# Up projection set up ahead of ten token tiles of the output projection, sample attention behind them

## The chip, the cores and the metric

The kernel runs on one core of a Trainium2 chip. The time is device microseconds (us) of that core for one execution. The kernel before took 2938.07 us, the median of 3 runs (2932.61 to 2941.27).

## What is computed

One decoder layer on 2064 prompt tokens (2048 and 16 learned ones ahead of them) and 32 sample tokens (8 sequences of 4, each with 2048 cached tokens in pages). Cut to what matters here:

```
q, k, v, u = split(rmsnorm(x, norm1) @ w_in)
ssm  = glu(S5(u))                                  # 512 columns
attn = head_norm(diff_attention(q, k, v))          # 512 columns, prompt
attn_sample = head_norm(diff_attention(q, [cache_k[pages], k], [cache_v[pages], v]))
x  = x + concat(attn, ssm) @ w_out                 # 1024 x 1024
xn = rmsnorm(x, norm2)
h  = gelu(causal_dwconv3(xn @ w_gate)) * (xn @ w_up)   # 1024 -> 2816, twice
y  = x + h @ w_down
```

All in float32: each large product is made of three matmuls over two fp32r parts of each operand (`mm3`, L80 to L82), so one operation of the text above is three PE instructions.

## The kernel before

The 2096 tokens lie in 17 tiles of 128 rows. Tile 16 has the last 48: 16 prompt tokens and the 32 sample tokens. The program is written stage by stage in `run` (L1580 ff.), and a scheduler (`schedule_with_timeline_sim=True`) puts the instructions of each engine in order: what is written earlier has priority, and what is written later is moved ahead where its own simulation finds an engine free and the buffers of the later stage are there. So the order in the text of `run`, and which pool of buffers opens where, set the order of the work. The pools lie in two stacks, one on each side of the memory, and a pool that takes the place of an earlier one waits for what was in it.

The stages that the change touches, in the order of the kernel before:

- `attend`, the prompt's attention, with work of lower priority beside it: `out_ssm` (the SSM half of the output projection of all tiles), `out_setup` (weights of the attention half, by `load_w_out`, L1111) and `out_attention(range(6))`, the other half for tiles 0 to 5.
- `out_attention(range(6, 16), ahead=True)`, the ten tiles 6 to 15, in pools of their own: `oax` with two buffers of each tile and `oap` with four banks of PSUM. A token tile takes two steps. `out_heads` (L1185 to L1208) loads three parts (`oxt`, and `ot` twice), multiplies and splits them on POOL and ACT, does 24 matmuls into two PSUM tiles `po` and stores the sum. `out_norm` (L1210 to L1240) norms it (`normed`, L161, with the scratch tile `xs`), transposes it (`tp`), and stores quarters of it and their differences in `XB`, from which the up projection reads. With `ahead` the norm of a tile is written behind the heads of the next.
- `up_setup` and `load_up` (L1288 ff.), which begin `ffn_up`: products `g` of tokens `xb` and weights `uw` (raw weights `uraw`), 128 columns of features a unit, 22 units in each of three blocks of token tiles: 0 to 5, 6 to 11, 12 to 16. A unit has seven products of quarter matrices (Strassen-Winograd), 12 matmuls each. A block cannot begin before all its tiles are in `XB`; the third needs tile 16.
- `sample_attention`, whose pools `smc` and `smw` open ahead of the ten tiles. It fetches the cache by gathers that POOL issues (L607): tiles `kv`, three buffers, 128 x 1024 float32 each, 64 gathers of keys and 64 of values. Keys are transposed on PE (`tps`), split and multiplied with the queries; after each half of the keys comes a softmax (`Ss`, L656 ff.); values are split by ACT (`vh`, L686) and DVE (`vl`, L688) and multiplied; the heads' sums (`att`, L699) are normed, transposed and put into `OT`, where tile 16 reads them.
- `out_setup` again, for tile 16, and `out_attention([16])`: the weights are loaded once more, in halves of 512 columns, each `oraw` through the one buffer with the tag "ot".
- `ffn_up`, which in the order of the engines runs beside the sample attention and tile 16, then `ffn_down`.

## Time and profile before

| | |
|---|---|
| median of 3 runs | 2938.07 us (2932.61 to 2941.27) |
| profiled execution, its own time | 2936.48 us |
| its span | 2934.7 us |
| granted clock of PE, mean of the span | 0.973 |
| PE (matmul) busy | 2750.9 us, 94% |
| PEld (weight load) busy | 2364.0 us, 81% |
| DVE busy | 2225.7 us, 76% |
| ACT busy | 1403.3 us, 48% |
| POOL busy | 1000.8 us, 34% |

Times inside the execution are us from the start of the span. A granted clock of 1.00 is the full 2.4 GHz of PE. Busy shares are means over the span: stages differ, so the table by stretches, further down, says more. L163 is line 163 of the kernel before; `po<-owh,oa` is an instruction that writes tile po and reads owh and oa. "x4" is a count, ACTq or SP a queue from which transfers are issued, "tile: min/median/max" are durations in ns.

### The profile page before, as it was taken

The page shows a single profiled execution, that of the slowest core. Times are in us where ns is not written, and L with a number is a line of the kernel's source. Part 1 is how long each engine was busy: PE and PEld are TensorE (multiplying, and loading weights), DVE is VectorE, ACT ScalarE, POOL GpSimd, SP SyncE. Part 2 cuts the span into 40 slices and gives each one's busy share as a digit, 9 for nine tenths or more (in the row PEclk, how much of TensorE's full clock was granted, in tenths as well). Part 3 has the DMA queues.
Part 4 walks back from the last instruction along what each step waited for, and adds up shares of the span by engine and source line. Part 5 has one row for each costly group of instructions (what it writes and reads, how often), then busy time and mean ns, then how long its engine had stood idle before and what let it go on. Part 6 is the DMA issues. An engine that isn't in the chain of part 4 may idle for free.

```text
span 2934.7 us, 43647 instructions
## 1 busy us (share of the span) xinstructions
PE 2750.9 (94%) x14916; PEld 2364.0 (81%) x14916; DVE 2225.7 (76%) x4317; ACT 1403.3 (48%) x2859; POOL 1000.8 (34%) x1381
## 2 busy tenths in 40 slices
PE   6989989979999899787999999999999998999999
PEld 6966667867887777676998998988999997778776
DVE  6748876757678898557898878898889994675566
ACT  3323223545556666335566556665565562222234
POOL 4525442115445576564243432343214441000000
PEclk9999999989999999999999999999999999999999
DMA  7876776977864332587455546454454447676554
GB/s 224 255 194 149 205 216 168 236 216 195 230 182 141 116 113 83 166 266 228 156 161 186 160 145 213 145 181 159 133 168 130 127 125 290 216 245 195 178 190 132
DMA packets 452553, 529.73 MB, mean 181 GB/s; under 512 B 91546, under 2 KB 353578, under 8 KB 451305
## 3 DMA queue, kind: packets, MB, share of 16 engines
q1 hardware_dynamic: 360584, 385.75, 45.0%
q10 hardware_dynamic: 72848, 72.79, 7.5%
q0 software_dynamic: 18896, 68.39, 7.4%
q8 instruction: 118, 1.93, 0.3%
q14 instruction: 107, 0.87, 0.1%
HBM read 390.49 MB, written 135.14 MB: 179 GB/s over the span
## 4 chain that ended last, share of the span: by engine, by line
PE 55%; DVE 9%; DMA 8%; POOL 2%; issue 2%; ACT 2%; SPq 0%; ACTq 0%; POOLq 0%; DVEq 0%
PE g L80 8%; PE g L81 8%; PE g L82 8%; PE pq L80 4%; PE pq L81 4%; PE pq L82 4%; PE O L537 3%; DVE p L507 2%; DMA ot<-RR 2%; PE po L80 1%; DMA oraw<-in_w_out_dram 1%; DMA dt<-MT 1%; PE po L81 1%; PE po L82 1%; PE tps L632 1%
## 5 line engine op out<-in xcount | busy, mean ns | idle before, releaser
L80 PE MATMUL g<-xb,uw 128*128 128x384 f32 (+1 forms) x1848 | 594.0, 324 | 8.8 <-DVE A L1408 4.8
L81 PE MATMUL g<-xb,uw 128*128 128x384 f32 (+1 forms) x1848 | 595.8, 323 | 1.2 <-DVE xb L69 1.2
L82 PE MATMUL g<-xb,uw 128*128 128x384 f32 (+1 forms) x1848 | 584.7, 322 | 0.4 <-DVE uw L69 0.4
L80 PEld LDWEIGHTS g<-xb,uw 128*128 128x128 f32 x1848 | 346.8, 188 | 19.3 <-DVE A L1408 5.3
L81 PEld LDWEIGHTS g<-xb,uw 128*128 128x128 f32 x1848 | 347.9, 188 | 9.1 <-issue 2.3
L82 PEld LDWEIGHTS g<-xb,uw 128*128 128x128 f32 x1848 | 346.1, 188 | 7.0 <-issue 1.2
L475 ACT ACTIVATE p<-S,nms 128x484 f32<-128x484 f32 (+11 forms) x360 | 210.1, 589 | 157.6 <-DVE nms L474 136.0
L80 PE MATMUL pq<-dw,da 128*128 128x512 f32 x616 | 245.9, 401 | 19.6 <-ACT da L68 11.8
L69 DVE TENSOR_TENSOR uw<-uraw,uw 128x512 fp32r<-128x512 f32 x330 | 239.5, 734 | 26.7 <-ACT uw L68 24.7
L68 ACT ACTIVATE uw<-uraw 128x512 fp32r<-128x512 f32 x330 | 201.0, 625 | 114.6 <-PE g L82 77.2
L81 PE MATMUL pq<-dw,da 128*128 128x512 f32 x616 | 245.5, 399 | 0.0
L82 PE MATMUL pq<-dw,da 128*128 128x512 f32 x616 | 236.9, 398 | 0.0
L474 DVE TENSOR_REDUCE nms<-S 128x1 f32<-128x484 f32 (+11 forms) x360 | 190.9, 554 | 40.9 <-PE S L469 27.4
L68 ACT ACTIVATE da<-dt 128x1024 fp32r<-128x1024 f32 x66 | 69.8, 1058 | 249.4 <-PE pq L82 149.3
L95 POOL TENSOR_TENSOR rs_y<-rs_v,half 128x8 f32<-128x8 f32 (+4 forms) x77 | 105.8, 1377 | 243.9 <-DVE rs_v L90 225.9
L80 PE MATMUL pj<-wh,x 128*128 128x512 f32 (+1 forms) x408 | 170.6, 419 | 8.1 <-ACT wh L74 5.7
L81 PE MATMUL pj<-wl,x 128*128 128x512 f32 (+1 forms) x408 | 170.3, 417 | 2.7 <-DVE wl L75 2.6
L82 PE MATMUL pj<-wh,x 128*128 128x512 f32 (+1 forms) x408 | 169.6, 416 | 0.0
L468 PE MATMUL S<-kt,qs 128*128 128x484 f32 (+11 forms) x360 | 145.7, 407 | 23.3 <-ACT p L475 13.5
L1311 POOL TENSOR_TENSOR uraw<-uraw 128x512 f32<-128x512 f32 x66 | 108.0, 1637 | 160.6 <-DVE s L1309 112.4
L80 PEld LDWEIGHTS pq<-dw,da 128*128 128x128 f32 x616 | 117.2, 190 | 50.5 <-ACT da L68 12.7
L505 POOL TENSOR_TENSOR p<-p,g 128x412 f32<-128x412 f32 (+13 forms) x164 | 156.5, 983 | 3.4
(423 smaller groups left out, 6895.7 us busy)
## 6 DMA issues: line engine op xcount, KB each, us to landing
dt<-MT SPq DMA_DIRECT2D x99, 512.0 KB
uraw<-in_w_gate_dram SPq DMA_DIRECT2D x66, 512.0 KB
uraw<-in_w_up_dram SPq DMA_DIRECT2D x66, 512.0 KB
raw<-in_w_in_dram SPq DMA_DIRECT2D x80, 256.0 KB
MT<-z ACTq DMA_DIRECT2D x44, 384.0 KB
dT<-in_w_down_dram SPq DMA_DIRECT2D x66, 256.0 KB
qs<-QST SPq DMA_DIRECT2D x128, 128.0 KB
draw<-in_w_down_dram SPq DMA_DIRECT2D x55, 256.0 KB
```

The costliest lines, as they stand in the source:

```text
L68: nc.scalar.activation(hi, src, AF.Copy)
L69: nc.vector.tensor_tensor(out=lo, in0=src, in1=hi.bitcast(F32), op=ALU.subtract)
L80: mm(out, lhsT=lh, rhs=rh, start=start, stop=False, skip_group_check=goes_on)
L81: mm(out, lhsT=lh, rhs=rl, start=False, stop=False, skip_group_check=goes_on)
L82: mm(out, lhsT=ll, rhs=rh, start=False, stop=stop, skip_group_check=goes_on)
L95: nc.gpsimd.tensor_tensor(out=y, in0=v, in1=e, op=ALU.pow)
L468: nc.tensor.matmul(dst, lhsT=qs[:, 0, c, qa : qa + M], rhs=kt[c][:, x:y], start=True, stop=False)
L474: nc.vector.tensor_reduce(out=nms[:M, z : z + 1], in_=dst, axis=AX.X, op=ALU.max, negate=True)
L475: nc.scalar.activation(p[:M, Z + x : Z + y], dst, AF.Exp, bias=nms[:M, z : z + 1], accum_out=sms[:M, z : z + 1])
L505: nc.gpsimd.tensor_tensor(out=pw[1][:M, x], in0=pw[1][:M, x], in1=g[:M, z : z + 1].to_broadcast([M, x.stop - x.start]), op=ALU.mult)
L537: nc.tensor.matmul(O[:, :N], lhsT=v, rhs=tw[:, m - a, :N], start=(m == 0), stop=(m == nb))
L1311: gp.tensor_tensor(out=a21, in0=a11, in1=a21, op=ALU.subtract)
```

## The change

The stages are written in another order: after the attention stand `up_setup`, with its pools and the products' PSUM, then the ten token tiles, and then the sample attention, whose pools `smc` and `smw` now open behind the ten tiles. The ten tiles use a pool with one buffer of each tile (`oax`, 1) and the PSUM pool of the up projection (`psf`) in place of one of their own. To make room the scratch tiles of the norm share buffers: `xs` and `xt1` with `ot`, `xod` with `oa`; the weights of both halves of the output projection share the buffers `owh0` to `owh3` and `owl0` to `owl3`, in one pool `oac` on the right. The option `ahead` is gone: a tile's norm is written right behind its heads. Nothing is computed in another way.

```diff
--- before.py
+++ after.py
@@ -61,6 +61,7 @@
 class Step:
     def __init__(self, tc, ins, outs):
         self.tc, self.nc, self.i, self.o = tc, tc.nc, ins, outs
+        self.tags = {"xs": "xs", "xod": "xod"}
     def split(self, hi, lo, src):
@@ -161,7 +162,7 @@
     def normed(self, wp, xt, n, g):
         nc = self.nc
-        xs = wp.tile([P, D], F32, name="xs", tag="xs")
+        xs = wp.tile([P, D], F32, name="xs", tag=self.tags["xs"])
         ss = wp.tile([P, 1], F32, name="ss", tag="ss")
         nc.scalar.activation(xs[:n], xt[:n], AF.Square, accum_out=ss[:n])
         r = self.rsqrt(wp, ss[:n], [n, 1], 1.0 / D, EPS, "xr")
@@ -1116,8 +1117,8 @@
         for k in range(k0, k0 + H):
             raw = wp.tile([P, n], F32, name="oraw", tag="ot")
             nc.sync.dma_start(out=raw, in_=i["w_out"][0, k * P : (k + 1) * P, c])
-            a = cp.tile([P, n], F32R, name="owh", tag=f"owh{k}")
-            b = cp.tile([P, n], F32R, name="owl", tag=f"owl{k}")
+            a = cp.tile([P, n], F32R, name="owh", tag=f"owh{k % H}")
+            b = cp.tile([P, n], F32R, name="owl", tag=f"owl{k % H}")
             if gain is None:
                 self.split(a, b, raw)
             else:
@@ -1160,27 +1161,18 @@
         else:
             self.w_att = lambda hf: self.load_w_out(0, cp, wp, gsub, slice(512 * hf, 512 * hf + 512))
-    def out_attention(self, tiles, wp, pp, ahead=False):
-        prev = None
+    def out_attention(self, tiles, wp, pp):
         for t in tiles:
-            xt = self.out_heads(t, wp, pp)
-            if ahead:
-                if prev:
-                    self.out_norm(*prev, wp, pp)
-                prev = t, xt
-            else:
-                self.out_norm(t, xt, wp, pp)
-        if prev:
-            self.out_norm(*prev, wp, pp)
+            self.out_norm(t, self.out_heads(t, wp, pp), wp, pp)
     def out_heads(self, t, wp, pp):
         nc, gp = self.nc, self.nc.gpsimd
@@ -1216,8 +1208,10 @@
         last = t == NT - 1
         m = n // 2 if last else P
         if t % 2 == 0:
-            self.quarters = [wp.tile([P, 2, 4, P], F32, name="x" + s, tag="x" + s) for s in ("ev", "od")]
-        ev, od = self.quarters
+            self.even = wp.tile([P, 2, 4, P], F32, name="xev", tag="xev")
+        ev, od = self.even, None
+        if t % 2 or last:
+            od = wp.tile([P, 2, 4, P], F32, name="xod", tag=self.tags["xod"])
         for b in range(2):
             tp = self.half_T(pp, xs, n, b)
             for z, x in enumerate((ev, od)) if last else ((0, (ev, od)[t % 2]),):
@@ -1229,7 +1223,7 @@
         if t % 2 == 0:
             keep(0, ev[:, :, :, :m], 2)
         if t % 2 or last:
-            t1 = wp.tile([P, 2, 4, P], F32, name="xt1", tag="xs")
+            t1 = wp.tile([P, 2, 4, P], F32, name="xt1", tag=self.tags["xs"])
             keep(2, od[:, 1:2, :, :m])
             gp.tensor_tensor(out=t1[:, 0, :, :m], in0=od[:, 0, :, :m], in1=ev[:, 0, :, :m], op=ALU.subtract)
             gp.tensor_tensor(out=t1[:, 1, :, :m], in0=od[:, 1, :, :m], in1=t1[:, 0, :, :m], op=ALU.subtract)
@@ -1645,28 +1639,32 @@
                             self.glu(gc, gw, pb)
                         self.project_kvq(kept, xq, wp, wq, pm, pa)
             with ExitStack() as fill:
+                oc = fill.enter_context(pool("oac", 1, side="right"))
                 with ExitStack() as att:
                     e = att.enter_context
                     fil = e(pool("fil", 1, space=PSUM))
                     ps = e(pool("ats", 1, space=PSUM, side="right"))
                     pools = [e(pool(nm, n, side="right")) for nm, n in (("atk", 4), ("atw", 2), ("atc", 1), ("atp", 7))]
                     self.attend(pools, ps)
-                    with pool("osc", 1) as oc, pool("osw", 2) as ow:
+                    with pool("osw", 2) as ow:
                         self.out_ssm(oc, ow, fil)
-                    oc = fill.enter_context(pool("oac", 1))
                     with pool("oaw", 1) as ow:
                         self.out_setup(oc, ow, 1)
                         self.out_attention(range(6), ow, fil)
                 up = ExitStack()
                 e = up.enter_context
                 pb = e(pool("psf", 4, space=PSUM, side="right"))
-                sam = ExitStack()
-                sc, sw = [sam.enter_context(pool(nm, n, side="right")) for nm, n in (("smc", 1), ("smw", 2))]
-                with pool("oax", 2) as ow, pool("oap", 4, space=PSUM, side="right") as pa:
-                    self.out_attention(range(6, 16), ow, pa, ahead=True)
-            pg = up.enter_context(pool("fg", 4, space=PSUM, side="right"))
-            fx, self.fr, self.fw, self.fz = [up.enter_context(pool(nm, 1)) for nm in ("fx", "fr", "fw", "fz")]
-            self.up_setup(fx, pg, pb)
+                pg = e(pool("fg", 4, space=PSUM, side="right"))
+                fx, self.fr, self.fw, self.fz = [e(pool(nm, 1)) for nm in ("fx", "fr", "fw", "fz")]
+                self.up_setup(fx, pg, pb)
+                with pool("oax", 1, side="right") as ow:
+                    self.tags = {"xs": "ot", "xod": "oa"}
+                    self.out_attention(range(6, 16), ow, pb)
+                    self.tags = {"xs": "xs", "xod": "xod"}
+            sam = ExitStack()
+            sc, sw = [sam.enter_context(pool(nm, n, side="right")) for nm, n in (("smc", 1), ("smw", 2))]
             self.sample_attention(sc, sw, pb)
             sam.close()
             with pool("obc", 1, side="right") as oc, pool("obw", 1, side="right") as ow:
```

On PE, at the end of the attention (`o_11820` and `rs_y` are its last sums; `po` belongs to the output projection, `g` to the up projection; from the fourth row on, the kernel before goes on with the rows of `po` of ten tiles, transposes of the norm and the beginning of the sample attention, until its first `g`):

```order
L552 MATMUL SS<-ones,o_11820 128x1 x8
L564 MATMUL tpr<-ident,rs_y 8x128
L80 MATMUL po<-owh,oa 128x512
L81 MATMUL po<-owl,oa 128x512
L82 MATMUL po<-owh,oa 128x512
L80 MATMUL po<-owh,oa 128x512
```

The same place in the change, the last two groups of the 24 rows of `po` of tile 6 and what follows:

```order
L82 MATMUL po<-owl,oa 128x512
L83 MATMUL po<-owh,oa 128x512
L81 MATMUL po<-owh,oa 128x512
L82 MATMUL po<-owl,oa 128x512
L83 MATMUL po<-owh,oa 128x512
L81 MATMUL g<-xb,uw 128x384
L82 MATMUL g<-xb,uw 128x384
L81 MATMUL g<-xb,uw 128x384
```

The first product `g` moved ahead of nine of the ten tiles and of all of the sample attention. The other nine tiles stand between products of the first block.

On POOL, around the last gathers (`kv`) of the sample attention, before:

```order
L607 DMA kv<-in_cache_v_dram,idx 128x1024 x4
L1311 TENSOR_TENSOR uraw<-uraw 128x4x128
L607 DMA kv<-in_cache_v_dram,idx 128x1024
L1434 COPY A<-carry 128x2
L607 DMA kv<-in_cache_v_dram,idx 128x1024 x3
L1436 COPY carry<-A 128x2
L1311 TENSOR_TENSOR uraw<-uraw 128x4x128
L607 DMA kv<-in_cache_v_dram,idx 128x1024
L1434 COPY A<-carry 128x2
L1436 COPY carry<-A 128x2
```

and in the change:

```order
L608 DMA kv<-in_cache_k_dram,idx 128x1024 x4
L1430 COPY carry<-A 128x2
L619 MEMSET qbd 128x1088
L625 COPY qbd<-qhl 64x4x4 x8
L608 DMA kv<-in_cache_k_dram,idx 128x1024 x13
L608 DMA kv<-in_cache_v_dram,idx 128x1024 x3
L646 MEMSET qn 128x544
L651 COPY qn<-qTs 64x4x4 x8
L608 DMA kv<-in_cache_v_dram,idx 128x1024 x29
L96 TENSOR_TENSOR rs_y<-rs_v,half 32x4
```

Before, single gathers stand between steps of the up projection (`uraw` are its weights, `A` and `carry` its convolution) to the end. In the change the last 45 gathers stand together, with no step of the up projection between them.

On SP, at tile 16 (`oraw` are rows of w_out, `oxt` and `ot` the tile's parts, `uraw` weights of the up projection, `xraw` the tokens of its third block), before:

```order
L1296 DMA uraw<-in_w_gate_dram 128x4x256 x2
L717 DMA OT<-saT 128x4x32
L1296 DMA uraw<-in_w_up_dram 128x4x256
L1153 DMA g_17234<-in_norm_dram 128x1024
L1155 DMA gsub<-in_sub_norm_dram 128x1
L1190 DMA oxt<-X_104 48x1024
L1192 DMA ot<-OT 128x4x48
L1195 DMA ot<-RR 128x4x48
L1296 DMA uraw<-in_w_up_dram 128x4x256
L1118 DMA oraw<-in_w_out_dram 128x512 x2
L1296 DMA uraw<-in_w_gate_dram 128x4x256
```

and in the change:

```order
L693 DMA vn<-VNS 32x512 x4
L718 DMA OT<-saT 128x4x32
L1154 DMA g_17226<-in_norm_dram 128x1024
L1156 DMA gsub<-in_sub_norm_dram 128x1
L1182 DMA oxt<-X_104 48x1024
L1184 DMA ot<-OT 128x4x48
L1187 DMA ot<-RR 128x4x48
L1119 DMA oraw<-in_w_out_dram 128x512 x8
L1276 DMA xraw<-XB 128x2x280 x3
```

The loads of weights of the up projection that stood between the steps of tile 16 are no longer there; the third block's tokens follow right behind it. On PE of the change, rows 8769 to 8998 hold no `g` at all, and 36 products of the second block stand behind them.

## Rows read from the trace of the kernel before

**Rows 1.** The page, its first line.
```profile
span 2934.7 us, 43647 instructions
```

**Rows 2.** Stretches: us; busy us of PE, PEld, DVE, ACT, POOL; PEclk; DMA share; GB/s.
```profile
1221.00:1357.00 136.00, 108.53 (x512) 89.19 (x513) 74.11 (x120) 48.73 (x88) 72.89 (x74) 0.88 0.82 254
1357.00:2056.00 699.00, 691.20 (x3890) 630.51 (x3890) 600.47 (x878) 420.66 (x698) 253.28 (x265) 1.00 0.53 169
2056.00:2196.00 140.00, 137.93 (x793) 133.94 (x792) 116.10 (x177) 75.99 (x135) 28.51 (x33) 1.00 0.51 156
2196.00:2442.00 246.00, 240.79 (x1853) 239.33 (x1852) 238.35 (x505) 145.89 (x291) 106.13 (x134) 0.99 0.41 126
```

**Rows 3.** Tiles tpr and g: ns min/median/max, first and last start in us.
```profile
L564 PE MATMUL tpr<-ident,rs_y x4: 271/273/373, 1003.7 to 1221.1; 128*8 128x128 f32 x4
...
L80 PE MATMUL g<-xb,uw x1848: 285/334/446, 1356.8 to 2442.1; 128*128 128x384 f32 x123, 128*128 128x280 f32 x62
```

**Rows 4.** Up products alone, PE, in 50 us of block 1.
```profile
2142.00:2192.00 50.00, 50.00 (x293) 1.00 0.47 154
```

**Rows 5.** Tile kv: durations of what consumes a value gather, and landing.
```profile
L686 ACT ACTIVATE vh<-kv x64: 1040/1060/1064, 1472.1 to 2028.8; 128x1024 fp32r<-128x1024 f32 x64
...
L688 DVE TENSOR_TENSOR vl<-kv,vh x64: 1202/1218/2558, 1473.2 to 2029.9; 128x1024 fp32r<-128x1024 f32 x64
...
DMA to landing us min/median/max: 4.2/5.4/12.4
```

**Rows 6.** Order of time, POOL: start us, us, instruction; six gathers.
```profile
1327.86 0.99 POOL L607 DMA_INDIRECT kv<-in_cache_k_dram,idx  x1 [6.98 <-PE tps L632]
...
1340.69 0.99 POOL L607 DMA_INDIRECT kv<-in_cache_k_dram,idx  x1 [0.42 <-PE tps L632]
...
1349.18 0.96 POOL L607 DMA_INDIRECT kv<-in_cache_k_dram,idx  x1 [2.52 <-PE tps L632]
...
1356.57 1.33 POOL L607 DMA_INDIRECT kv<-in_cache_k_dram,idx  x1 [5.20 <-PE tps L632]
...
1981.19 1.82 POOL L607 DMA_INDIRECT kv<-in_cache_v_dram,idx  x1 [4.04 <-DVE swT L69]
...
2023.36 1.72 POOL L607 DMA_INDIRECT kv<-in_cache_v_dram,idx  x1 [2.88 <-DVE vl L688]
```

**Rows 7.** Tile Ss: softmax of the sample attention.
```profile
L656 DVE TENSOR_REDUCE snm<-Ss x2: 2305/2312/2320, 1485.9 to 1882.0; 128x1 f32<-128x2080 f32 x2
...
L658 ACT ACTIVATE Ss<-Ss,snm x2: 2038/2038/2039, 1490.9 to 1884.3; 128x2080 f32<-128x2080 f32 x2
```

**Rows 8.** Order of time: last head product, and last store of tile 16.
```profile
2044.41 1.04 PE L699 MATMUL att<-om,sel 64*32 64x512 f32 x2
...
2129.06 0.37 ACTq L1227 DMA_DIRECT2D XB<-xev  x1
```

**Rows 9.** Chain of waits that ended last, 2060 to 2200: start us, us, what.
```profile
2061.99 5.11 DMA ot<-RR
...
2068.99 2.54 DMA oraw<-in_w_out_dram
...
2097.27 0.73 ACT owh L74
...
2098.03 0.76 DVE owl L75
...
2102.80 4.53 DMA oraw<-in_w_out_dram
...
2192.37 4.38 DMA xraw<-XB
```

**Rows 10.** Stretch with the fastest transfers; columns as in rows 2.
```profile
2450.00:2500.00 50.00, 47.24 (x195) 37.94 (x196) 16.12 (x17) 13.61 (x17) 0.00 (x0) 0.94 1.03 393
```

**Rows 11.** Order of time, ACT queue: stores of two tiles beside the attention.
```profile
1061.40 0.34 ACTq L1207 DMA_DIRECT2D X<-oxt  x1
...
1176.35 0.34 ACTq L1207 DMA_DIRECT2D X<-oxt  x1
```

## The prediction

> **What bounds the kernel now.** I read the table of stretches first, then where each stretch begins and ends, then the waits inside the stretch that the change takes apart. The profiled execution spans 2934.7 us [rows 1]; its own time is 2936.5 us, 1.6 us under the median of the three runs, so the sum below is made against it and 1.6 us is added at the end. The stretches behind the attention [rows 2] show four regimes. From the last attention product at 1221.1 to the first up product at 1356.8 [rows 3], 136 us pass in which PE is busy for 109 us and the granted clock averages 0.88: ten token tiles of the output projection, and the beginning of the sample attention. From 1357 to 2056 the up projection runs interleaved with the sample attention, PE is busy for 691 of 699 us at clock 1.00, and DVE for 600. From 2056 to 2196 the up projection goes on alone, while the last token tile (16) is projected and normed beside it. From 2196 on the third block of the up projection runs with DVE busy for 238 of 246 us, and the down projection follows. So between 1357 and 2196 PE is the bound, and in the 136 us ahead of it nothing is.
>
> **What is moved, and its gain.** The ten tiles no longer stand ahead of the up projection but inside its first block, and the sample attention begins only behind them. In the new order of PE the first up product follows directly on the last attention rows and one projection tile (24 matmuls). That tile costs 4 us at the 0.18 us a matmul found below, so the up projection starts near 1225 instead of 1357: 132 us earlier. Its first operands come from the first six tiles, as before, and those are done beside the attention. The PE work of the stretch does not vanish, it is put between up products. The new order has 4740 PE instructions from the first up product to the last one ahead of the place I call the tail: 3660 up products, 406 cache transposes, 200 score products, 216 projection products, 80 transposes of the norm, 136 value products and some 40 small ones. The old stretch 1357 to 2056 did 3890 of very nearly this mixture in 699 us [rows 2], so 0.1797 us each with all waits in it; 4740 x 0.1797 = 852 us. The tail begins at 1225 + 852 = **2077**. I take that price rather than the 50.0/293 = 0.171 us of up products alone [rows 4], which is the lower bound (809 us, tail at 2034).
>
> **What it uncovers.** At that point the first two blocks of the up projection are finished but for 36 products, and the sample attention is not: 13 key gathers, all scores of the second half behind them, 32 value gathers, and tile 16 remain. On POOL they stand as 13 + 3 + 29 gathers with no work for the up projection between them, and on PE no up product stands until the transposes of tile 16. The third block cannot start earlier either: its tokens are tiles 12 to 16, and tile 16 holds the sample tokens. Before, all of this lay beside up products and cost only its PE share. Now its latency is on the path:
>
> - Key gathers. Three buffers serve pairs of gathers, and a pair's buffers come free with its last transposes. With PE nearly free the pairs followed each other after 8.5 and 7.4 us [rows 6]: 6.5 pairs x 8.0 = 52 us. The lower bound is the same with the shortest landing instead of the median, 1.2 us less each [rows 5], 44 us; the upper one is the step just before, 12.8 us beside projection products, 83 us.
> - Softmax of the second half. The reduction takes 2.3 us and the exponential 2.0 [rows 7]; with the table load, the scaling, 17 transposes, ten small splits and the handovers I estimate 13 us (10 to 30).
> - Value gathers. A buffer is held for landing 5.4 + copy 1.06 + subtraction 1.22 = 7.7 us [rows 5], and there are three: 2.56 us each, 32 x 2.56 = 82 us. With the shortest landing, 4.2 us, it is 69 us. The upper bound is the pace beside the up projection: ten steps from 1981.2 to 2023.4 [rows 6], 4.2 us each, 135 us. I stay near the lower end, because ACT and DVE have nothing else to do in the tail.
> - A second set of transposed weights, and from the last gather to the head products: 8 us.
> - Tile 16. From the last such product at 2044.4 to its last store at 2129.1 took 85 us beside the up projection [rows 8]. Of this the eight loads of its projection weights, one after the other through one buffer, are 2069.0 to 2107.3, 38 us; alone each needs landing 2.5, copy 0.73 and remainder 0.76 [rows 9], 32 us together. The other 46 us are short steps and four transfers with queueing; I take 38. Sum 70 us (60 to 85).
> - Store, load (4.4 us [rows 9]) and split of the third block's first tokens, which before had been far ahead of need: 8 us.
>
> Together 52 + 13 + 82 + 8 + 70 + 8 = 233 us. The third block begins at 2077 + 233 = 2310, where it began at 2196: 114 us later. The 36 left up products (6 us) run beside the last transfers. Everything behind is the same work: 2936.5 + 114 + 1.6 = **3052 us**. SP's queue costs nothing in the first block: nine sets of three tile loads stand between weight loads that run a unit ahead. In the tail SP has nothing else to load.
>
> Of the clock the rows show 0.88 in the 136 us where PE was busy for four fifths, and 1.00 where it was busy throughout [rows 2]. In the tail PE has some 360 instructions in 233 us. At the lower level (1.2 of 2.4 GHz) the part of a key pair's PE work that lies in its chain (12 of 24 instructions, 2.2 us) would double: +14 us, which I leave to the range. The Trainium skill ("TensorE: Matmul & The Clock Gate", Part 1) says that the slow clock is the default and activity lifts it; by that rule the tail runs slow and the time is 3066 us.
>
> **The rivals.**
> A. The single-buffered projection cannot keep up with the up products, and PE waits at its rows in the first block. The new order has 1593 PE instructions for nine tiles, 177 or 32 us each. Beside the attention, with single buffers, tiles stored their rows at 1061.4, and three tiles later at 1176.4 [rows 11]: 38 us each. 38 - 32 = 6 us x 9 = +57: 3109 us, and more (3154 us) if the next tile's loads, 5.1 us [rows 9], are not hidden either, since the norm's scratch now shares their buffer. Against it: in the attention the order of PE itself spread these products out, and POOL, which has eight or so steps a tile, was busy for 73 of 136 us with ten tiles and the first gathers and for 253 of 699 us beside the up projection [rows 2], so both together fit.
> B. The gathers land faster when nothing else moves. With 4.2 instead of 5.4 us [rows 5], 8 + 13 = 21 us less: 3031 us. For it: the tail has no other large transfer. Against it: three gathers are in flight together. The Trainium skill ("DMA: Bandwidth & Descriptors", Anatomy of one DMA, SWDGE path) gives 2.0 us plus bytes at 436 GB/s, which would be an estimate of 3.2 us for 512 KB and a time of 3014 us; no gather of this trace comes near it.
> C. Not slower: the waits overlap fully and each stretch runs at the pace of its busiest resource, PE ahead of the tail and the DMA engines in it. The tail begins at 2034, and 45 gathers of 512 KB at 393 GB/s [rows 10] take 1.33 us each, 60 us, with 13 + 4 + 64 + 8 behind them: the third block begins at 2183, and the time is 2925 us. It decides when the tail is shorter than 2196 - 2034 = 162 us. Against it: with three buffers 1.33 us a gather would need 4 us from issue to free, and the landing alone is 4.2 at best.
>
> **How the numbers follow.** The forecast, with its terms between their nearer bounds, has 0.60 and covers about 3015 to 3090. A has 0.17, B 0.14, C 0.04; 0.05 is left for a tail as slow as it was beside the up projection (83 + 30 + 135 + 12 + 85 + 10 = 355 us, 3174 us). The range 2990 to 3135 holds the forecast, A and B. A measurement of this kernel tells 0.3%, 9 us, from no change; only C and what lies below it is not slower: faster 0.03, same 0.02, slower 0.95.
>
> **What would show it.** Right: the first up product near 1225; PE dense at clock 1.00 until about 2080; then over 200 us in which PE is busy for less than a third, value gathers about 2.6 us apart, no up product; the third block beginning near 2310; the down projection as long as before. A shows as waits of PE for the projection's operands between 1230 and 1550. The forecast is wrong if value gathers come under 2 us apart or the tail is shorter than 160 us, and most of all if up products run inside it.

## The result: 3.65% slower, third block later as forecast

The changed kernel took 3048.8 us, the median of 4 runs (3038.61 to 3052.86); the kernel before, beside it, 2939.67 us (2932.61 to 2947.23). The ratio is 1.0365, with a 95% interval of 1.034 to 1.039. The profiled execution took 3052.86 us over a span of 3051.1 us, 116.4 us more than that of before.

The page of the changed kernel, its first line and the busy time of each engine:

```profile
span 3051.1 us, 43684 instructions
...
PE 2791.6 (91%) x14916; PEld 2374.1 (78%) x14916; DVE 2234.1 (73%) x4317; ACT 1412.5 (46%) x2859; POOL 971.9 (32%) x1381
```

PE has 41 us more busy time than before (2750.9) for the same work, and the span is 116 us longer. The table of stretches, columns as in [rows 2], cut at the points that the prediction names: the first up product, the end of the tiles, the beginning of the tail, then the pieces of the tail, then the third block:

```profile
1226.00:1540.00 314.00, 313.48 (x1746) 302.41 (x1747) 253.06 (x394) 155.61 (x272) 114.69 (x102) 0.99 0.50 158
1540.00:2068.00 528.00, 523.23 (x3005) 484.85 (x3004) 427.59 (x638) 304.26 (x511) 178.79 (x206) 1.00 0.51 165
2068.00:2122.00 54.00, 35.69 (x162) 25.67 (x160) 21.32 (x33) 18.00 (x32) 12.17 (x13) 0.87 0.39 125
2122.00:2140.50 18.50, 4.82 (x27) 3.86 (x27) 8.93 (x14) 7.33 (x14) 4.94 (x13) 0.59 0.38 118
2140.50:2227.00 86.50, 64.11 (x160) 23.95 (x161) 46.52 (x56) 36.76 (x47) 27.86 (x27) 0.68 0.54 166
2227.00:2288.00 61.00, 21.07 (x49) 8.23 (x50) 13.11 (x27) 8.69 (x16) 4.39 (x9) 0.50 0.22 57
2288.00:2305.60 17.60, 7.64 (x27) 6.76 (x27) 10.65 (x14) 11.52 (x19) 2.21 (x3) 0.60 1.02 330
2305.60:2558.00 252.40, 247.22 (x1851) 244.68 (x1851) 243.16 (x506) 149.50 (x292) 91.45 (x133) 0.99 0.39 127
```

The first two lines answer to the second line of [rows 2]: PE is dense at clock 0.99 and 1.00, first with the ten tiles beside the up projection and then with the sample attention beside it. From 2068 on it is not: the five lines from 2068 to 2305.6 hold 133 us of busy time in 238 us, and the granted clock falls as far as 0.50, the lower of the two levels. The last line answers to the last of [rows 2]: the third block again has DVE busy for nearly its whole length, and takes 252 us instead of 246.

The first up product stands at 1226.0 (1356.8 before [rows 3]), the last one ahead of the gap at 2067.7, the next at 2284.4. The chain of waits through that gap, as start, length and what it was, of the view that [rows 9] shows for the kernel before:

```profile
2080.74 4.37 DMA kv<-in_cache_k_dram,idx
...
2113.43 4.53 DMA kv<-in_cache_k_dram,idx
...
2121.01 1.21 PE Sp L639 x4
2122.31 5.48 DMA kv<-in_cache_v_dram,idx
...
2215.77 5.30 DMA kv<-in_cache_v_dram,idx
2221.17 1.06 ACT vh L687
2222.26 1.24 DVE vl L689
2223.53 0.69 PE os L682
...
2226.89 1.93 PE att L700 x2
...
2243.42 2.61 DMA oraw<-in_w_out_dram
2246.11 0.73 ACT owh L75
2246.86 0.76 DVE owl L76
...
2272.79 2.63 DMA oraw<-in_w_out_dram
...
2287.94 4.10 DMA XB<-xev
...
2292.43 4.65 DMA uraw<-in_w_gate_dram
```

All of it was there before, beside up products. Now nothing else runs beside these pieces, and the chain goes through them: key gathers one after the other, value gathers and their splits, the head sums, eight loads of output weights, the third block's operands.

### The profile page after: what moved, and what is told of

The parts are those of the page before. It is cut to its first block, busy times and chain, and to the rows that moved or that the text cites. A ratio compares the mean times of both kernels' runs of the same rounds, so it can differ in the third digit from the quotient of the medians.

```text
span 3051.1 us, 43684 instructions
## 1 busy us (share of the span) xinstructions
PE 2791.6 (91%) x14916; PEld 2374.1 (78%) x14916; DVE 2234.1 (73%) x4317; ACT 1412.5 (46%) x2859; POOL 971.9 (32%) x1381
## 4 chain that ended last, share of the span: by engine, by line
PE 54%; DMA 9%; DVE 8%; issue 4%; ACT 2%; POOL 2%; ACTq 0%; SPq 0%; POOLq 0%; DVEq 0%
PE g L83 8%; PE g L81 8%; PE g L82 8%; PE pq L81 4%; PE pq L82 4%; PE pq L83 4%; PE O L538 3%; DVE p L508 2%; PE po L81 2%; PE po L82 2%; PE po L83 2%; DMA kv<-in_cache_v_dram,idx 2%; DMA dt<-MT 1%; PE tpw L531 1%; PE S L469 1%
## 5 line engine op out<-in xcount | busy, mean ns | idle before, releaser
L81 PE MATMUL g<-xb,uw 128*128 128x384 f32 (+1 forms) x1848 | 597.5, 327 | 19.7 <-ACT uw L69 17.7
L81 PEld LDWEIGHTS g<-xb,uw 128*128 128x128 f32 x1848 | 351.0, 191 | 27.4 <-ACT uw L69 19.9
L82 PEld LDWEIGHTS g<-xb,uw 128*128 128x128 f32 x1848 | 352.3, 191 | 4.7 <-issue 1.2
L83 PEld LDWEIGHTS g<-xb,uw 128*128 128x128 f32 x1848 | 348.4, 190 | 7.0 <-DVE uw L70 3.5
L475 DVE TENSOR_REDUCE nms<-S 128x1 f32<-128x484 f32 (+11 forms) x360 | 190.6, 556 | 36.7 <-PE S L470 25.6
L508 DVE SCALAR_TENSOR_TENSOR p<-p,f 128x412 f32<-128x412 f32 (+13 forms) x164 | 147.6, 914 | 19.2 <-POOL p L506 19.1
```

Of the source, the lines that this page charges most:

```text
L81: mm(out, lhsT=lh, rhs=rh, start=start, stop=False, skip_group_check=goes_on)
L82: mm(out, lhsT=lh, rhs=rl, start=False, stop=False, skip_group_check=goes_on)
L83: mm(out, lhsT=ll, rhs=rh, start=False, stop=stop, skip_group_check=goes_on)
L475: nc.vector.tensor_reduce(out=nms[:M, z : z + 1], in_=dst, axis=AX.X, op=ALU.max, negate=True)
L508: nc.vector.scalar_tensor_tensor(out=w[:M, x], in0=w[:M, x], scalar=fs[0][:M, z : z + 1], in1=pw[1][:M, x], op0=ALU.mult, op1=ALU.add)
```

## The experiments

The theory: the loss is the latency of the sample attention's last part and of tile 16, which no longer has up products beside it, less the earlier start. Its rivals: the projection with single buffers holds up PE in the first block (A of the prediction); the low clock of the tail lengthens it; the gathers are slow in themselves. Two lengths are compared besides the medians: from the last attention product to the third block (975.2 us before, 1092.1 changed), and inside the tail. The third block is counted from the 3697th product `g`, since each block has 1848; a few of its own products stand 7 to 8 us ahead of that, mixed with the last ones of the second block, in both kernels. These lengths are free of what differs between executions ahead of them: the attention's first product came anywhere from 633 to 651 us in the profiled executions of these kernels.

### What a step in the tail costs, and what the same step costs before

Sixteen of the last 32 value gathers go, in both kernels:

```diff
-                for r in range(8):
+                for r in range(8 if sq < 4 else 4):
                     vt = gather("cache_v", sq, r)
```

In the changed kernel:

> The changed kernel without 16 of the last 32 value gathers (sequences 4 to 7 use the first half of their cached values), with their splits and value products. Theory: in the tail the gathers are the path, at 3.1 us each (28 gathers from 2131.1 to 2215.8), so 16 x 3.1 = 50 us go: 2990 to 3010 us. Rival (the tail is bound by something else, the slow clock of PE or the handovers of tile 16): only the PE work goes, 64 products at 0.2 to 0.4 us, 13 to 26 us at most: 3020 to 3040 us.

3006.92 us, ratio to before 1.0232 (1.0182 to 1.0281): 41.9 us less than the changed kernel. The stretch from the first value product to the last head sum of the second half:

```profile
2139.20:2182.90 43.70, 33.76 (x95) 13.70 (x95) 27.02 (x40) 19.51 (x32) 12.37 (x11) 0.73 0.47 137
```

It was 86.5 us with 32 gathers and is 43.7 with 16: 2.7 us a gather. The theory holds for the value gathers. The 3.1 us expected here were too many, since they counted the wait for the second set of weights, and the 2.56 us of the prediction were the better figure. In the kernel before:

> The kernel before without the same 16 value gathers, their splits and value products. Theory (there the gathers lie beside up products, PE is the bound and only their PE work counts): 64 products at 0.213 us are 14 us, so 2918 to 2932 us. Rival (a gather costs its latency in any order): 40 to 50 us go, 2888 to 2898 us.

2921.13 us, 0.9944 (0.9923 to 0.9965): 14.6 us less, about the 14 us of PE time that the 64 products were expected to take. The same gathers cost 42 us in one order and 15 in the other.

Four buffers for tile 16's output weights, in both kernels:

```diff
-            raw = wp.tile([P, n], F32, name="oraw", tag="ot")
+            raw = wp.tile([P, n], F32, name="oraw", tag="ot" if n == D else "oraw", bufs=None if n == D else 4)
```

> The changed kernel with four buffers instead of one for the rows of the output weights that tile 16 loads again. Theory: their eight loads and splits, now 2243.4 to 2277.1 one after the other, are on the path; with four buffers the loads overlap and the splits (1.5 us each) remain, 12 to 15 us: 18 to 24 us are gained, 3022 to 3034 us. Rival (the path runs elsewhere, in the token loads and the norm of tile 16): no change, within 9 us of 3049.

3016.28 us, 1.0282 (1.0236 to 1.0328). The loads and splits of this run, as queue or engine, count, ns and first and last start:

```profile
L1119 SPq DMA_DIRECT2D oraw<-in_w_out_dram x8: 327/330/505, 2224.6 to 2233.5; - x8
L75 ACT ACTIVATE owh<-oraw,gsub x8: 706/722/724, 2230.0 to 2237.1; 128x512 fp32r<-128x512 f32 x8
L76 DVE SCALAR_TENSOR_TENSOR owl<-oraw,gsub,owh x8: 735/747/754, 2230.7 to 2238.5; 128x512 fp32r<-128x512 f32 x8
```

They take from 2224.6 to 2239 instead of 2243.4 to 2277. The stretch from the last head sum to the third block:

```profile
2213.70:2266.80 53.10, 23.29 (x74) 15.41 (x75) 23.29 (x41) 19.73 (x35) 6.61 (x11) 0.60 0.58 175
```

It was 78.7 us, so the gain there is 25.6 us of the 32.5 in the medians; the rest lies in other stretches. The gain is more than the 18 to 24 us expected. The loads now start 11 us behind the last head sum instead of 16.5, since the first four have buffers of their own and no longer wait for the tile's own loads to be used.

> The kernel before with the edit of the run that gave the changed kernel four buffers for tile 16's output weights. Theory (there the same loads lie beside up products and are not on the path): within 9 us of 2938. Rival (those loads cost as much in any order): 18 to 32 us are gained, as in the changed kernel.

2935.67 us, 0.9984 (0.9966 to 1.0003): no change. One edit, 26 us in the tail and nothing beside up products. That is the theory's difference between the two orders, shown twice.

### The low clock of the tail

Zero matmuls beside the last 32 value gathers, so that PE does not rest there:

```diff
                         pv(r * 2 + t, P, vh[:, t], vl[:, t])
+                        for _ in range(WARM if sq >= 4 else 0):
+                            nc.tensor.matmul(os_, lhsT=none, rhs=wT[:, 0:4].rearrange("p a b c d -> p (a b c d)"), start=False, stop=False)
```

Eight for each gather (WARM = 4):

> The changed kernel with eight more matmuls for each of the last 32 value gathers, which add zero to the sums (a block of zeros as weights), so that PE does not rest while the values are gathered. Nothing is left out. Theory (gathers set the pace, PE's clock does not): 8 x 0.21 = 1.7 us a gather beside 0.85 of its own is less than the 3.1 us a gather takes, so the time stays within 10 us of 3049, though the granted clock between 2137 and 2225 rises from 0.6 to 0.7 to over 0.9. Rival (the low clock lengthens each step of the tail): the steps shorten and 15 to 30 us are gained.

3059.91 us, 1.0435 (1.0387 to 1.0483), 11 us slower than the changed kernel, just outside the 10 us expected. The stretch from first value product to last head sum:

```profile
2126.00:2230.90 104.90, 101.16 (x416) 55.92 (x416) 46.85 (x56) 36.55 (x47) 26.39 (x27) 0.94 0.45 138
```

PE is busy for nearly all of it: the four value products and eight zero matmuls of a gather became the pace, and the run doesn't answer the question. With two for each gather (WARM = 1):

> The changed kernel with two zero matmuls more for each of the last 32 value gathers instead of eight: 0.43 us at the high clock, 0.85 at the low one, beside 0.85 to 1.5 of its own. With eight, PE was busy for 88 of 91 us and became the pace itself. Theory (gathers set the pace): within 12 us of 3049, at most as much slower as 32 x 0.4 us, whatever the clock does. Rival (the low clock lengthens the tail): 15 to 30 us are gained if the granted clock between 2134 and 2225 rises above 0.9.

3047.34 us, 1.0367 (1.0347 to 1.0386), the same as the changed kernel. The same stretch:

```profile
2137.10:2225.10 88.00, 66.38 (x223) 29.41 (x223) 46.52 (x56) 36.46 (x47) 27.71 (x27) 0.89 0.54 163
```

The granted clock rose from 0.68 to 0.89, just short of the 0.9 that the expectation asked for, and the value products became shorter, with medians of 0.40 us instead of 0.63; but the stretch went from 86.5 to 88 us. In the value part the clock is not what sets the pace. In the key part and in tile 16, where it was 0.87 and 0.50, it wasn't tried.

### The change's way of doing the tiles, by itself

The kernel before with the change's way of doing the ten tiles, but in the old place, ahead of the up projection. That is more than the buffers: one buffer of each tile, the shared scratch, the PSUM pool of the up projection, and each norm right behind its heads (of the edit, the lines that use the shared tags are left out here):

```diff
...
-                with pool("oax", 2) as ow, pool("oap", 4, space=PSUM, side="right") as pa:
-                    self.out_attention(range(6, 16), ow, pa, ahead=True)
+                with pool("oax", 1) as ow:
+                    self.tags = {"xs": "ot", "xod": "oa"}
+                    self.out_attention(range(6, 16), ow, pb)
+                    self.tags = {"xs": "xs", "xod": "xod"}
```

> One part of the change alone: the kernel before with the ten tiles in the order of heads and norm of the change, with one buffer of each tile, the shared scratch and the PSUM pool of the up projection, but ahead of the up projection as before. Theory: a tile then takes the 27 to 38 us between tiles that the changed kernel shows, instead of 9 to 10, so ten take 250 to 350 us instead of 136; sample attention runs beside them and takes some of that back, so the first up product comes 100 to 200 us later and the time is 2990 to 3090 us: in the change this price is paid by up products beside the tiles, and hidden. Rival (single buffers cost little anywhere): within 20 us of 2938.

3097.04 us, 1.0548 (1.0525 to 1.057), 7 us over the range expected. The tiles took from 1219 to 1473; a first key gather was issued at 1218.7, but the first cached keys were transposed only at 1464.6, so hardly any sample attention ran beside the tiles, which the expectation had counted on. PE's waits in that stretch (total us, times, longest):

```profile
PE po L81 <- ACT oa L1199: 93.3, 9, 13.2
PE tp L180 <- DVE xs L172: 58.1, 10, 9.5
```

The waits of PE in the changed kernel while it does the same tiles beside up products:

```profile
PE g L81 <- ACT uw L69: 4.9, 1, 4.9
PE po L81 <- ACT oa L1190: 0.5, 1, 0.5
```

151 us of waits for the two tiles that share buffers, against 0.5. So the price of this way of doing the tiles is real, 118 us here in the stretch (254 instead of 136), and in the change up products hide it. Rival A of the prediction names a real cost that has cover. How much of it is the single buffers and how much the order of heads and norms isn't told apart.

### Cover given back to the tail

If the loss is missing cover, holding products of the up projection back until the sample attention has got further should return it. Each product of the first two blocks, from the 125th on, is put behind a given step of the sample attention in PE's order, by an edge that orders issue and waits for nothing (`marks` is a list that the sample attention fills, of a weight in us and an instruction: 4.5 for a pair of key gathers, 15 for a softmax, 2.1 for a value gather, 10 for the end; a product has 2.1, `PER`, and `HELD` is 124):

```diff
+    def hold(self):
+        self.count = getattr(self, "count", -1) + 1
+        at, end, ins = (self.count - HELD) * PER, 0, None
+        for us, x in self.marks:
+            end += us
+            if end > at:
+                break
+            ins = x or ins
+        return self.tc.issue_after(ins.ins) if ins and self.count < 2 * 22 * 7 else nullcontext()
```

> The changed kernel with one thing more: from the 125th product on, each product of the first two blocks of the up projection is put on PE behind a given step of the sample attention (one product for each value gather, two for each pair of key gathers, seven for a softmax), in issue order alone, with no wait. The same work, the same buffers. Theory (the loss is latency of the sample attention and tile 16 that has no up product left beside it): PE is busy again through the whole of it, the third block begins at 2150 to 2210 instead of 2306, and the time is 2895 to 2955 us, no slower than the kernel before. Rival 1 (the projection with single buffers holds up the first block): nothing in that is changed, at most 10 us are gained. Rival 2 (gathers slow beside the up projection, 4.2 us a value gather as in the kernel before): PE now waits in its order for gathers; 128 gathers of which each is 1 to 2 us late give 100 to 200 us back, so 3000 us or more.

3015.47 us, 1.0283 (1.0235 to 1.0331): 33 us of the 109 between the medians came back, so this expectation missed. The time lies where its second rival, slow gathers, had put it. The third block begins at 2263.6. PE's waits between 1600 and 2200:

```profile
PE Sp L644 <- DVE kT L74: 19.0, 26, 2.1
PE Sp L644 <- ACT kT L73: 16.3, 15, 2.4
PE tps L638 <- DMA kv<-in_cache_k_dram,idx: 9.2, 3, 3.2
```

The order of PE's instructions is fixed when the kernel is built. With the products in twelves, each key's transposes had to be split before PE could go on, and with three buffers one gather of a pair came late. Slow gathers are not what these rows show: the waits for gathers are 9 us of the 77 that PE was idle. A wait there costs more than itself. PE in time order, as start and length, with rows of the same kind left out:

```profile
1907.44 0.44 PE L638 MATMUL tps<-ident,kv 128*128 128x128 f32 x2 [2.96 <-DMA kv<-in_cache_k_dram,idx]
...
1907.98 0.53 PE L85 MATMUL g<-xb,uw 128*128 128x384 f32 x1
1908.31 0.53 PE L86 MATMUL g<-xb,uw 128*128 128x384 f32 x1
...
1911.42 0.33 PE L87 MATMUL g<-xb,uw 128*128 128x384 f32 x1
1911.60 0.33 PE L85 MATMUL g<-xb,uw 128*128 128x384 f32 x1
```

Behind this wait of 2.96 us the products start 0.31 to 0.33 us apart until 1911.2, and then 0.17 to 0.18. The granted clock was 1.00 from 1900 to 1907.4, 0.50 from 1908.0 to 1911.1, and 1.00 again from 1911.6 on.

In threes, with four buffers for tile 16's output weights:

> The changed kernel with the up products held back as in the first such run, but in threes instead of twelves, and with four buffers for tile 16's output weights. In the first such run PE still waited 78 us between 1600 and 2200, for splits of keys and for gathers behind which nothing else stood, and the third block began at 2264. Theory: threes cover the waits for splits (35 us there) and the buffers take some 25 us off tile 16, so 2955 to 2985 us; the waits for key gathers with three buffers stay. Rival (what is left is not latency but the transfers themselves or the clock): 2995 us or more.

2986.61 us, 1.0158 (1.0121 to 1.0194), just over the range expected. It is 29 us less, about what the weight buffers alone gave; PE's idle time between 1600 and 2200 fell from 77 to 61 us, so the threes brought less than expected. With a fourth gather buffer as well:

```diff
-            kt = wp.tile([P, 2, 512], F32, name="kv", tag="kv", bufs=3)
+            kt = wp.tile([P, 2, 512], F32, name="kv", tag="kv", bufs=4)
...
-            w = self.fw.tile([P, 2, 4, P], F32R, name="uw", tag="uw", bufs=7)
+            w = self.fw.tile([P, 2, 4, P], F32R, name="uw", tag="uw", bufs=6)
```

> The same with four gather buffers instead of three, and six buffers instead of seven for split weights of the up projection, to make the room. Theory (two pairs of key gathers can be under way, so PE no longer waits for one): another 20 to 40 us less than with three, 2920 to 2960 us, about the kernel before. Rival (seven weight buffers are needed, PE waits for weights instead): as with three or slower.

2945.05 us, 1.0034 (1.0015 to 1.0053), as expected. The third block begins at 2192.7, and what PE still waits for between 1600 and 2190 is small and no gather:

```profile
PE att L708 <- DVE om L706: 6.1, 6, 2.2
PE Sp L644 <- DVE kT L74: 5.7, 7, 1.5
PE tps L723 <- DVE asum L719: 5.6, 1, 5.6
PE tps L680 <- DVE swT L74: 5.4, 4, 4.1
```

The last of the held kernels gets the room from smaller constants, so the split weights have seven buffers again, and keeps products for these places. QBD and ATT are further marks with their own weights, and the weights of a pair of keys, a softmax and the end are lowered to 3.4, 12 and 8 us. Of its edit, the constants:

```diff
-        bm = cp.tile([64, 512], F32, name="bm")
+        bm = cp.tile([64, H], F32, name="bm")
...
-        sel = cp.tile([64, NS, 32], F32, name="sel")
+        sel = cp.tile([64, 60], F32, name="sel")
...
-        aT = wp.tile([P, H, 32], F32, name="saT", tag="saT", bufs=1)
+        aT = wp.tile([P, H, 32], F32, name="saT", tag="sl", bufs=1)
```

> The changed kernel with the up products held back in threes, four gather buffers, four buffers for tile 16's output weights and again seven for the split weights of the up projection; the room comes from smaller constants (the head mask as 64 x 4 and broadcast, the selection as one window of 64 x 60, the last transposed sums in a shared buffer). Some more products are kept for the places where PE still waited: the block queries, the new keys, the head sums, and tile 16. Theory: PE was idle for 41 us between 1520 and 2200 with four buffers, and the low clock behind its gaps cost some more; half of it goes, and the third block is as fast as before: 2905 to 2935 us, at or below the kernel before. Rival (what PE saves in waits comes back at the end, as gathers under way get slower): 2940 us or more.

2928.57 us, 0.997 (0.9957 to 0.9984): as expected, a little faster than the kernel before. All of the change's loss is gone, with the change's order of stages kept, so the theory stands. The weight buffers alone gave 32.5 us of it; no run has the fourth gather buffer in this order without the held products, so what these two bring by themselves is not told apart. But the stretches say that little else was won. Attention, tiles beside up products, sample attention beside up products, third block:

```profile
646.00:1207.40 561.40, 526.17 (x2891) 434.52 (x2892) 463.59 (x1151) 337.05 (x1022) 301.72 (x605) 0.98 0.54 159
1207.40:1520.00 312.60, 306.34 (x1681) 292.68 (x1682) 247.51 (x372) 154.22 (x267) 105.52 (x96) 0.98 0.52 161
1520.00:2184.90 664.90, 629.54 (x3514) 559.70 (x3513) 541.65 (x816) 392.11 (x650) 254.02 (x275) 0.98 0.59 187
2184.90:2429.50 244.60, 240.38 (x1853) 239.21 (x1852) 237.84 (x504) 145.56 (x291) 106.06 (x134) 0.99 0.41 126
```

From the last attention product to the third block 977.5 us pass, 975.2 before. PE was idle, as length less busy time, for 42 us of them here and for 37 there. The attention itself, however, takes 561 us here and 578 before: that is where this kernel is ahead. The control for it, the same buffers in the old order:

> The kernel before with the buffers of the best version (four gather buffers, four for tile 16's output weights, the smaller constants), in its own order and with no products held back. Theory (PE is the bound there from the first up product on, and the gathers lie beside it): no change, 2928 to 2944 us, so that what the best version gains comes from the earlier up projection together with the held products. Rival (the fourth gather buffer is what helps, in any order): 2915 us or less.

2927.74 us, 0.9965 (0.9951 to 0.9979): just as fast. It lies 0.3 us below what was expected as no change, and its interval says that it is a little faster than the kernel before. So the old order with more buffers does as well as the early up projection with held products, and no gain needs the new order. The two do not win in the same place: here the attention is not shorter, 585 us, and the 968.9 us from there to the third block are 6 us less than before. But the profiled execution was this run's slowest, 2940.33 us, so where its 9 us come from stays open.

## Why the prediction was right

Forecast 3052, measured 3048.8. Term by term, from the profiled execution:

| step | forecast | measured |
|---|---|---|
| first up product | 1225 | 1226.0 |
| beginning of the tail | 2077 | 2067.7 |
| key gathers to the last score | 52 | 54.5 (2067.7 to 2122.2) |
| softmax and first weights | 13 | 18.3 (to 2140.5) |
| value gathers, second weights, head sums | 90 | 86.4 (to 2226.9) |
| tile 16 | 70 | 61.0 (to its last store, 2287.9) |
| store, load and split for the third block | 8 | 9.9 to its first product (2297.8), 17.7 to its counted start (2305.6) |
| tail | 233 | 237.9 |
| third block begins | 2310 | 2305.6 |

**The tail** is the step on which the result turned, and it was right as a mechanism and as a size; the two skip runs and the two runs with four weight buffers show it, for the value gathers and for tile 16's weights, as a price that only the changed order pays. The key gathers and the softmax were not taken out by themselves; for them the chain of waits and their lengths speak. Three terms were sized less well, and partly cancel: the softmax took 5 us more, tile 16 took 9 less, and the last step took 17.7 us instead of 8. Tile 16's projection loads took 34 us as forecast (32 to 38), so its other steps took less. In the last step the third block's first product, of 280 columns, waited for weights and not for tokens:

```profile
2297.78 0.60 PE L81 MATMUL g<-xb,uw 128*128 128x280 f32 x1 [9.20 <-ACT uw L69]
```

These weights came behind the tokens on SP's queue: the chain ends in a load of `uraw` at 2292.43, which the prediction did not count. The other 7.8 us hold 25 products, among them some of the 36 left ones. The forecast had put all 36 beside the last transfers; 12 ran there, from 2284.4 to 2288, and the other 24 came behind the wait.

One sign did not come. The prediction wanted PE busy for less than a third of the tail, and it was busy for 133.6 of 237.9 us, more than half. It had 424 instructions there against the 360 of the prediction and the 36 left products, and they took longer: 160 of them filled 64 of 86.5 us in the value part, 0.40 us each, at a granted clock of 0.68. Being busy did not set the pace there: in the run with two zero matmuls a gather these products became shorter and nothing was won.

**The price of a product beside sample work**, 0.1797 us, came out at 0.1776 (841.7 us for 4740), 10 us less in all.

**Three things the sum did not have** nearly cancel. The attention took 562.5 us instead of 578.1, and ended at 1213.5, though it began 8 us later in this execution. All nine kernels measured with the change's pools have such an attention (561 to 567 us), and all five with the old ones have the longer one (577 to 585). Below are the attention and the stretch from its last product to the third block, with the columns of [rows 2], first before and then changed:

```profile
643.00:1221.10 578.10, 538.29 (x2892) 441.29 (x2893) 459.23 (x1164) 333.94 (x1018) 306.15 (x608) 0.97 0.54 154
1221.10:2196.30 975.20, 937.95 (x5193) 853.89 (x5194) 790.98 (x1173) 545.38 (x920) 354.58 (x370) 0.98 0.57 179
```

```profile
651.00:1213.50 562.50, 530.45 (x2891) 437.56 (x2892) 463.06 (x1152) 337.51 (x1022) 302.45 (x605) 0.98 0.54 159
1213.50:2305.60 1092.10, 977.63 (x5194) 861.51 (x5195) 789.12 (x1182) 547.86 (x916) 345.23 (x371) 0.92 0.50 159
```

PE has the same instructions in the first stretch, and 8 us less busy time. The prediction took everything ahead of 1221 as unchanged; the order inside the attention changed too (the first products of the output projection stand 13 us behind the attention's first one, 21 before). Which part of the change does it wasn't tried, beyond that the ten tiles' own buffers don't (581 us with those alone). The third block took 252.4 us instead of 246.1, where "the same work" was forecast. The 116.4 us between the two profiled executions are so: 8.1 of the later beginning, −15.6 of the attention, 116.9 from there to the third block (forecast: 113.9), 6.3 of that block, and 0.7 behind it. The stretch that the prediction worked out is off by 3 us, and there is luck in that: from the last attention product to the first up product 12.5 us passed where 4 were allowed, the products ahead of the tail took 10 less, and the tail took 5 more. That the first up product came at 1226.0, with 1225 forecast, is luck too, since the shorter attention and this longer step cancel. That the whole is off by no more has luck in it as well.

**The rivals.** A (the projection holds up PE) is out: PE waited 0.5 us for it while the tiles were done. What it did wait for was the first weights, 4.9 of the 12.5 us between the attention and the first up product. B (gathers land faster when alone) is out by the landings in the tail:

```profile
DMA to landing us min/median/max: 4.1/5.1/5.6
```

The prediction took 5.4 as median and 4.2 as the least. The Trainium skill ("DMA: Bandwidth & Descriptors", Anatomy of one DMA) led to an estimate of 3.2 us for such a gather; no gather in the tail came under 4.1, and the measurement decides. C (no slower, each stretch at its busiest resource) is out with B: the tail lasted 238 us where C needed under 162.

**The clock.** The Trainium skill ("TensorE: Matmul & The Clock Gate", Part 1) has activity lift the clock from its slow default, and the tail agrees: the granted clock was 0.50 to 0.87 there. The 14 us that the prediction set aside for it in the key part did not show: the keys came within 3 us of their price, at a granted clock of 0.87, and the value part takes the same time at 0.68 and at 0.89. At the end, where PE itself is on the path, the clock does show: most of the products from 2297.8 to 2305.6 start 0.23 to 0.32 us apart at 0.50, where right behind 2306.3 they start 0.13 to 0.17 apart.

## What to carry to other kernels

In a stretch where one engine is the bound, an earlier start can win little more than that engine's idle time: 37 us of 975 here, which the last held kernel (42 of 977) did not lower. Before moving a long chain of transfers behind other work, count what is left to lie beside it at its end; here 36 products were left for 238 us of latency. A chain that costs only its share of the busy engine under cover can cost its whole latency without it, and the test is cheap: make the same cut in both orders and compare.

## What the runs showed of the hardware

A wait of PE can cost more than its length. In the first held kernel the products behind a wait of 2.96 us came 0.31 to 0.33 us apart at a granted clock of 0.50, where at 1.00 they come 0.17 to 0.18 apart. The products behind the 4.9 us wait at 1226 in the changed kernel did the same: mostly 0.32 us apart, at a granted clock of 0.50 from 1226 to 1230. From 1600 to 2200 that held kernel's granted clock was 0.94 on average, where the dense stretches of the changed kernel have 0.99 and 1.00. That is part of why it gave back only 33 us.

A low clock in a stretch whose pace the gathers set cost nothing that these runs show: 86.5 us at 0.68, 88 at 0.89, although the value products took 0.63 us at the one and 0.40 at the other.
